# Attention masks: from matmuls into PSUM to one VectorE pass that adds the mask, takes the maximum and writes SBUF

## The chip, the cores and the metric

The kernel runs on one core of one Trainium2 chip. Five engines work side by side, each with an instruction queue of its own that runs in order: TensorE (PE in the profile, with its weight loads as PEld) multiplies matrices and writes PSUM; VectorE (DVE) and ScalarE (ACT) do elementwise work on SBUF and PSUM; GpSimd (POOL) does elementwise work on SBUF; SyncE (SP) issues the DMAs of this kernel. They tell each other with semaphores when a result is there or a buffer is free.

The metric is the time of one execution on the device in microseconds (us). Before the change the median of three runs is 2638.52 us, the lowest 2634.18 and the highest 2640.28.

## What is computed

The reference is a decoder trunk of two layers on 1024 tokens of width 1024. Layer 0 mixes with "native sparse attention" of 12 heads: each head attends in three branches, to all earlier tokens (with 16 blocks of 64 tokens and the 16 best taken, every block is selected, so only the causal mask is left), to a window of 512 tokens, and to 63 compressed blocks. Layer 1 mixes with forgetting attention, causal as well, with a decay that is added to the scores. In both layers 4 more heads attend to 256 memory tokens, with no mask. A gated convolutional feed-forward part follows in each layer. What the change touches is the masked softmax:

```python
def masked_softmax(s, mask):
    s = jnp.where(mask, s, NEG)
    s = s - jnp.max(s, axis=-1, keepdims=True)
    e = jnp.exp(s) * mask
    return e / jnp.maximum(jnp.sum(e, axis=-1, keepdims=True), 1e-30)
...
        s = jnp.einsum('btghd,bngd->bghtn', qc, kc).astype(jnp.float32) * scale
        p_cmp = masked_softmax(s, cmp_end[None, :] <= t[:, None])
...
        p = masked_softmax(s.reshape(B, G, HG, Q_BLOCK, n_top * L_SEL), m_sel)
...
        m_win = (s_pos[None, :] >= 0) & (s_pos[None, :] <= t[:, None]) & (t[:, None] - s_pos[None, :] < WINDOW)
        s = jnp.einsum('btghd,bsgd->bghts', qc, kw).astype(jnp.float32) * scale
        p = masked_softmax(s, m_win)
...
        s = s + dcum[:, :, lo:hi, None] - dcum[:, :, None, :hi]
        p = masked_softmax(s, jnp.arange(hi)[None, :] <= t[:, None])
```

## The kernel before, in words

The kernel is one class, Trunk, that issues the whole program, with an order written out by hand in `attention`; a scheduler below it may move instructions within an engine's queue as their operands allow. Numbers are kept in 32 bits; a product of full precision is made of three matmuls on high and low parts (`mm3`, lines 156 to 158; `split`, lines 81 and 82).

Attention goes head by head. A unit is one head and one half c of the tokens (512 queries, as four blocks of 128, counted by `ii`). A unit of layer 0 has three branches: the causal one (tile `ps`), the window (`pw`) and the compressed blocks (`pc`), whose scores are made together with the window's ("joint": 64 more columns behind the window's). A unit of layer 1 has the causal branch alone; a memory unit (`pm` in layer 0) has 256 unmasked columns for each of its four blocks.

A branch is cut into groups of query blocks that fit two PSUM banks, the tile `psa` of 1024 columns, of which there are two. For each group:

- `score` (line 301) multiplies queries and keys into `psa`. Where a mask is needed, one more matmul adds it: the identity (`identb`, bf16) as weights, and as moving operand a mask of zeros and -1e30: `caub` (causal, 128 columns), `winb` (far edge of the window, 128 columns), or `wcb` (the causal mask of the window's last block and the mask of the 64 compressed blocks, 192 columns). Blocks that need no mask get no such matmul.
- `maximum` (lines 314, 318, 320): VectorE takes the negated maximum of each row from PSUM, into `stat`. Four unmasked blocks of equal width go in one instruction (line 314).
- `exponent` (lines 334, 337): ScalarE reads the scores from PSUM, adds the negated maximum as a bias, takes the exponential and writes the probabilities to the SBUF tile `ps`, `pw` or `pc`. An accumulator gives the row sums (ACTIVATION_READ_ACCUMULATOR); those of `pc` are summed on VectorE at line 341.
- `normalise` (lines 346 to 361): one over the sum on VectorE, then the scaling of the probabilities on GpSimd in layer 0 and mostly on VectorE in layer 1.

The units are worked off in steps. In a step, `turn_p` transposes up to four 128x128 pieces of probabilities on PE (line 391) into one of the four `psb` banks, ScalarE copies them to `pt` (line 398), VectorE makes the low part (`lower_p`, line 401), and two steps later `value` multiplies them with the values (line 414). `pace` sets at which step each group of scores is begun: several steps ahead of the first step that needs it, and not before the step that last uses the tile of probabilities that it will write (`early`). The maximum and the exponential of a group come one step after its scores: the maximum before that step's transposes, the exponential behind them.

```python
            run(k, "max")
            if st:
                self.turn_p(ap, st)
            run(k, "exp")
            if st:
                self.lower_p(st)
            run(k, "norm")
            while items and items[0]["at"] <= k:
                begin(k, items.pop(0))
```

Between the steps, projections of later heads are interleaved on PE as filler (`advance`), in both layers.

## Time and profile before

| what | value |
|---|---|
| median of three runs | 2638.52 us |
| the profiled execution, as timed | 2643.03 us |
| its span, first to last instruction | 2640.9 us |
| granted TensorE clock, mean | 0.985 |
| scores, L301, last seen in layer 0 and layer 1 | at 652 us and 1850 us |
| reductions L318 from PSUM | 288 instructions, 200.6 us |
| reductions L320 from PSUM (64 columns) | 96 instructions, 20.4 us |
| exponentials and their sums, L334 | 260.1 us |

How to read the profile. A row of the grouped view has the line of the kernel, the engine, the operation, output and inputs by the program's names, the shapes and the count; behind the first bar stand the busy time in us and the mean of one in ns, and behind the second the idle time of the engine just before these instructions and what ended it. Matmuls are pipelined, so the duration of one is longer than the time by which the next one follows it. The chain of waits goes back from the last instruction to what released it, step by step, and its shares tell which engines' work stood in the way of the end. A row of the waits has the waiting engine and line, what it waited for, the us in total, the number of times and the longest. In the timeline a row has the start, the duration and the instruction, and in brackets the idle time before it.

### The profile page before, as it was taken

The page shows a single profiled execution, that of the slowest core. Times are in us where ns is not written, and L with a number is a line of the kernel's source. Part 1 is how long each engine was busy: PE and PEld are TensorE (multiplying, and loading weights), DVE is VectorE, ACT ScalarE, POOL GpSimd, SP SyncE. Part 2 cuts the span into 40 slices and gives each one's busy share as a digit, 9 for nine tenths or more (in the row PEclk, how much of TensorE's full clock was granted, in tenths as well). Part 3 has the DMA queues.
Part 4 walks back from the last instruction along what each step waited for, and adds up shares of the span by engine and source line. Part 5 has one row for each costly group of instructions (what it writes and reads, how often), then busy time and mean ns, then how long its engine had stood idle before and what let it go on. Part 6 is the DMA issues. An engine that isn't in the chain of part 4 may idle for free.

```text
span 2640.9 us, 36023 instructions
## 1 busy us (share of the span) xinstructions
PE 2506.7 (95%) x12642; PEld 2073.0 (78%) x12642; DVE 1881.6 (71%) x2822; ACT 1331.5 (50%) x2553; POOL 751.2 (28%) x616
## 2 busy tenths in 40 slices
PE   7899899988999999998999999999999999998998
PEld 6787777776877888886888988887777888886886
DVE  5757677878377787877765467778576877787765
ACT  4437576768245454544454356656334545443443
POOL 0105344445133545543000000000223555454000
PEclk9999999999999999999999999999999999999999
DMA  8473123334422323337434556656532333337523
GB/s 243 142 206 109 53 81 100 89 108 136 153 88 82 102 96 109 108 125 273 133 128 128 160 171 194 188 177 181 197 112 69 104 112 100 101 105 262 186 90 118
DMA packets 302702, 357.72 MB, mean 135 GB/s; under 512 B 37961, under 2 KB 183225, under 8 KB 302521
## 3 DMA queue, kind: packets, MB, share of 16 engines
q1 hardware_dynamic: 302520, 355.41, 42.8%
q8 instruction: 100, 1.64, 0.3%
q14 instruction: 82, 0.66, 0.1%
HBM read 245.55 MB, written 109.78 MB: 135 GB/s over the span
## 4 chain that ended last, share of the span: by engine, by line
PE 71%; DVE 9%; DMA 6%; ACT 6%; POOL 4%; issue 3%; SPq 1%; POOLq 0%; ACTq 0%; DVEq 0%
PE psa L156 11%; PE psa L157 11%; PE psa L158 11%; PE psb L156 8%; PE psb L158 8%; PE psb L157 8%; PE psa L301 5%; PE psb L414 4%; PE psb L391 3%; DVE pt L401 2%; DVE stat L318 2%; POOL gs L1350 1%; DMA hT<-in_w_down_dram 1%; ACT ps L334 1%; POOL pw L358 1%
## 5 line engine op out<-in xcount | busy, mean ns | idle before, releaser
L81 ACT ACTIVATE wh<-wr 128x512 fp32r<-128x512 f32 (+2 forms) x254 | 193.1, 765 | 353.9 <-PE psb L158 147.2
L82 DVE TENSOR_TENSOR wl<-wr,wh 128x512 fp32r<-128x512 f32 (+2 forms) x254 | 241.6, 955 | 165.5 <-ACT wh L81 164.8
L1335 DVE SCALAR_TENSOR_TENSOR v<-u,cw,v 128x1023 f32<-128x1023 f32 (+1 forms) x176 | 273.1, 1552 | 68.7 <-ACT v L1333 65.8
L401 DVE TENSOR_TENSOR pt<-psb,pt 128x512 fp32r<-128x512 f32 (+2 forms) x380 | 245.7, 657 | 87.2 <-ACT pt L398 84.6
L398 ACT ACTIVATE pt<-psb 128x512 fp32r<-128x512 f32 (+2 forms) x380 | 217.5, 583 | 130.9 <-PE psb L391 129.5
L1333 ACT ACTIVATE v<-u,cw 128x1024 f32<-128x1024 f32 x88 | 109.6, 1245 | 310.2 <-DVE u L1322 283.4
L414 PE MATMUL psb<-pt,vv 128*128 128x512 f32 (+2 forms) x864 | 232.2, 366 | 12.4 <-DVE pt L401 9.0
L156 PE MATMUL psa<-hT,wh 128*128 128x512 f32 x560 | 219.2, 392 | 5.3 <-DVE u L1296 5.3
L301 PE MATMUL psa<-kk,qq 128*128 128x512 f32 (+4 forms) x792 | 196.4, 359 | 25.0 <-ACT ps L334 14.7
L158 PE MATMUL psa<-hT,wl 128*128 128x512 f32 x560 | 218.6, 390 | 0.8 <-DVE wl L82 0.8
L157 PE MATMUL psa<-hT,wh 128*128 128x512 f32 x560 | 218.5, 390 | 0.0
L318 DVE TENSOR_REDUCE stat<-psa 128x1 f32<-128x640 f32 (+7 forms) x288 | 200.6, 714 | 21.5 <-PE psa L301 20.3
L334 ACT ACTIVATE ps<-psa,stat 128x128 f32<-128x128 f32 (+2 forms) x224 | 156.7, 706 | 59.6 <-DVE stat L318 53.7
L120 POOL TENSOR_TENSOR rs<-ss,consts 128x1 f32<-128x1 f32 x44 | 25.8, 588 | 516.3 <-DVE ss L118 378.0
L472 POOL TENSOR_TENSOR wr<-wr 128x512 f32<-128x512 f32 x32 | 42.3, 1323 | 440.7 <-DMA wr<-o 426.6
L414 PEld LDWEIGHTS psb<-pt,vv 128*128 128x128 f32 x864 | 141.4, 195 | 30.8 <-DVE pt L401 16.1
L301 PEld LDWEIGHTS psa<-kk,qq 128*128 128x128 f32 x792 | 125.8, 194 | 47.3 <-ACT ps L334 23.6
L156 PE MATMUL psb<-hT,wh 128*128 128x512 f32 x384 | 160.0, 417 | 2.2 <-DVE rt L607 1.8
L156 PE MATMUL psb<-wh 128*128 128x512 f32 x352 | 139.3, 396 | 20.7 <-ACT wh L81 20.6
L1237 POOL TENSOR_TENSOR ws<-wr 128x512 f32<-128x512 f32 x44 | 74.7, 1699 | 295.6 <-DMA wr<-in_w_up_dram 213.2
L391 PE MATMUL psb<-consts,ps 128*128 128x128 f32 x928 | 150.7, 280 | 8.1 <-DVE pt L401 4.9
L158 PE MATMUL psb<-hT,wl 128*128 128x512 f32 x384 | 151.7, 395 | 0.0
(285 smaller groups left out, 6853.1 us busy)
## 6 DMA issues: line engine op xcount, KB each, us to landing
wr<-in_w_up_dram SPq DMA_DIRECT2D x88, 512.0 KB
wr<-gd SPq DMA_DIRECT2D x154, 256.0 KB
gd<-v SPq DMA_DIRECT2D x88, 256.0 KB
gd<-gs SPq DMA_DIRECT2D x66, 256.0 KB
o<-ob SPq DMA_DIRECT2D x128, 128.0 KB
wr<-o SPq DMA_DIRECT2D x32, 512.0 KB
hT<-in_w_down_dram SPq DMA_DIRECT2D x64, 256.0 KB
qd<-st SPq DMA_DIRECT2D x56, 256.0 KB
```

The source lines that it names most:

```text
L81: nc.scalar.activation(hi, src, AF.Copy)
L82: nc.vector.tensor_tensor(lo, src, f32(hi), ALU.subtract)
L156: mm(out, lh, rh, start=first, stop=False, skip_group_check=more)
L157: mm(out, lh, rl, start=False, stop=False, skip_group_check=more)
L158: mm(out, ll, rh, start=False, stop=last, skip_group_check=more)
L301: nc.tensor.matmul(out, w, rhs, start=b not in banks[:i], stop=b not in banks[i + 1:])
L318: nc.vector.reduce_max(br["stat"][:, 0, ii:ii + 1], s[:, o:o + w], axis=AX.X, negate=True)
L391: nc.tensor.transpose(tp[0:kb, x:x + P], br["pt"][ii][:, o:o + kb], self.ident)
L398: nc.scalar.activation(st["hi"], st["src"], AF.Copy)
L401: self.nc.vector.tensor_tensor(st["lo"], st["src"], f32(st["hi"]), ALU.subtract)
L414: self.nc.tensor.matmul(out, v, t, start=st["begin"] and i == 0, stop=st["end"] and i == len(mms) - 1)
L1335: nc.vector.scalar_tensor_tensor(v[:, d:], u[:, :S - d], cw[:, tap, i:i + 1], v[:, d:], ALU.mult, ALU.add)
```

## The change

The mask matmuls and the identity in bf16 are gone. The masks become as wide as the scores: `caub` has 1024 columns, of which the first 896 are zero and the last 128 hold the causal mask, and a block of n columns takes its last n; `winb` has five blocks of 128 (far edge, three of zeros, causal); `cmpb` holds 64 columns for each of the eight query blocks.

A new function, `lift`, issues one VectorE operation for each query block and branch that has a mask: it adds score (PSUM) and mask (SBUF), multiplies by -1, writes the result to the tile of probabilities in SBUF, and takes the minimum along the row into `stat`, which is the negated maximum. In the instruction list of the changed kernel each of these is followed by a second VectorE instruction of 128x1 that writes `stat`. The exponential then reads the tile of probabilities and writes it in place, with a scale of -1 and the same bias. The tile of probabilities is therefore claimed in `maximum` and no longer in `exponent`. Memory units, without a mask, keep the reduction and the exponential from PSUM.

VectorE has 3207 instructions in the changed program (2822 before). PE has the same 12304 other matmuls, and 336 mask matmuls fewer.

```diff
@@ -90,21 +90,22 @@
         nc.sync.dma_start(c, a["consts"][:, 0:C_CAU])
         self.ident = c[:, C_ID:C_ID + P]
         self.rv = c[:, C_RV:C_RV + 1]
-        self.identb = cp.tile([P, P], BF16, name="identb")
-        nc.vector.tensor_copy(self.identb, self.ident)
-        self.m_cau = cp.tile([P, P], BF16, name="caub")
+
+        self.m_cau = cp.tile([P, S], BF16, name="caub")
+        nc.vector.memset(self.m_cau[:, :S - P], 0.0)
         self.nhalf = c[:, C_NH:C_NH + 1]
 
     def masks(self, pool, keep):
         nc, m = self.nc, pool.tile([P, C_TRI - C_CAU], F32, name="masks")
         nc.sync.dma_start(m, self.a["consts"][:, C_CAU:C_TRI])
-        nc.vector.tensor_copy(self.m_cau, m[:, 0:P])
-        self.m_win = keep.tile([P, P], BF16, name="winb")
-        nc.vector.tensor_copy(self.m_win, m[:, P:2 * P])
-
-        self.m_wc = keep.tile([P, NT, 192], BF16, name="wcb")
-        nc.vector.tensor_copy(self.m_wc[:, :, P:], m[:, 2 * P:].rearrange("p (t n) -> p t n", t=NT))
-        nc.vector.tensor_copy(self.m_wc[:, :, 0:P], m[:, 0:P].rearrange("p (o n) -> p o n", o=1).to_broadcast([P, NT, P]))
+        nc.vector.tensor_copy(self.m_cau[:, S - P:], m[:, 0:P])
+
+        self.m_win = keep.tile([P, 5 * P], BF16, name="winb")
+        nc.vector.memset(self.m_win[:, P:4 * P], 0.0)
+        nc.vector.tensor_copy(self.m_win[:, 0:P], m[:, P:2 * P])
+        nc.vector.tensor_copy(self.m_win[:, 4 * P:], m[:, 0:P])
+        self.m_cmp = keep.tile([P, NT, 64], BF16, name="cmpb")
+        nc.vector.tensor_copy(self.m_cmp, m[:, 2 * P:].rearrange("p (t n) -> p t n", t=NT))
 
     def gain(self, pool, row, bufs=1):
         g = self.sb(pool, [P, D], F32, "gb", bufs)
@@ -279,7 +280,7 @@
         nc, br, s = self.nc, it["br"], self.psa()
         it["s"] = s
         for ii, o, n in it["grp"]:
-            k0, k1, masks = br["spans"][ii]
+            k0 = br["spans"][ii][0]
             if "joint" in br:
                 f, t0 = n - 192, k0 // P
                 segs = [(o + f, o + n, lambda k: k[:, t0 + f // P, :])]
@@ -294,8 +295,6 @@
                     rhs = at(k)
                     out = s[:, b0:b1] if len(rhs.shape) == 2 else s[:, b0:b1].rearrange("p (t n) -> p t n", n=P)
                     mms.append((b0 // CH, out, q[:, ii * P:(ii + 1) * P], rhs))
-            for mo, mk in masks:
-                mms.append(((o + mo) // CH, s[:, o + mo:o + mo + mk.shape[1]], self.identb, mk))
             banks = [b for b, *_ in mms]
             for i, (b, out, w, rhs) in enumerate(mms):
                 nc.tensor.matmul(out, w, rhs, start=b not in banks[:i], stop=b not in banks[i + 1:])
@@ -309,34 +308,43 @@
             for i, b in enumerate(u["branches"]):
                 b["stat"] = u["stat"][:, :, 4 * i:4 * i + 4]
         br["same"] = len({k1 - k0 for k0, k1, _ in br["spans"].values()}) == 1
-        if br["same"] and len(grp) == 4:
-            n = grp[0][2]
-            nc.vector.reduce_max(br["stat"][:, 0, :], s[:, 0:4 * n].rearrange("p (i n) -> p i n", n=n), axis=AX.X, negate=True)
-        else:
-            for ii, o, n in grp:
-                w = n - 64 if joint else n
-                nc.vector.reduce_max(br["stat"][:, 0, ii:ii + 1], s[:, o:o + w], axis=AX.X, negate=True)
-                if joint:
-                    nc.vector.reduce_max(joint["stat"][:, 0, ii:ii + 1], s[:, o + w:o + n], axis=AX.X, negate=True)
-
-    def exponent(self, ap, it):
-        nc, br, s = self.nc, it["br"], it["s"]
-        joint = br.get("joint")
         if it["first"]:
             for b in (br, joint) if joint else (br,):
                 tag, width, bufs = b["p"]
                 b["pa"], b["pt"], b["len"] = self.sb(ap, [P, width], F32, tag, bufs), {}, 0
+        if br["spans"][0][2] is None:
+            n = grp[0][2]
+            nc.vector.reduce_max(br["stat"][:, 0, :], s[:, 0:4 * n].rearrange("p (i n) -> p i n", n=n), axis=AX.X, negate=True)
+            return
+        for ii, o, n in grp:
+            w = n - 64 if joint else n
+            self.lift(br, ii, s[:, o:o + w])
+            if joint:
+                self.lift(joint, ii, s[:, o + w:o + n])
+
+    def lift(self, br, ii, s):
+
+        w = s.shape[1]
+        p = br["pt"][ii] = br["pa"][:, br["len"]:br["len"] + w]
+        br["len"] += w
+        self.nc.vector.tensor_tensor_reduce(p, s, br["spans"][ii][2], -1.0, 3e38, ALU.add, ALU.min, br["stat"][:, 0, ii:ii + 1])
+
+    def exponent(self, ap, it):
+        nc, br, s = self.nc, it["br"], it["s"]
+        joint = br.get("joint")
         for ii, o, n in it["grp"]:
-            w = n - 64 if joint else n
-            p = br["pa"][:, br["len"]:br["len"] + w]
-            br["pt"][ii] = p
-            br["len"] += w
-            nc.scalar.activation(p, s[:, o:o + w], AF.Exp, bias=br["stat"][:, 0, ii:ii + 1], accum_out=br["stat"][:, 1, ii:ii + 1])
+            st = br["stat"]
+            if br["spans"][ii][2] is None:
+                p = br["pt"][ii] = br["pa"][:, br["len"]:br["len"] + n]
+                br["len"] += n
+                nc.scalar.activation(p, s[:, o:o + n], AF.Exp, bias=st[:, 0, ii:ii + 1], accum_out=st[:, 1, ii:ii + 1])
+                continue
+            p = br["pt"][ii]
+            nc.scalar.activation(p, p, AF.Exp, bias=st[:, 0, ii:ii + 1], scale=-1.0, accum_out=st[:, 1, ii:ii + 1])
             if joint:
-                p = joint["pt"][ii] = joint["pa"][:, ii * 64:(ii + 1) * 64]
-                nc.scalar.activation(p, s[:, o + w:o + n], AF.Exp, bias=joint["stat"][:, 0, ii:ii + 1])
-                joint["len"] += 64
-        if joint and joint["len"] == 256:
+                p = joint["pt"][ii]
+                nc.scalar.activation(p, p, AF.Exp, bias=joint["stat"][:, 0, ii:ii + 1], scale=-1.0)
+        if joint and it["last"]:
             joint["same"] = True
             nc.vector.reduce_sum(joint["stat"][:, 1, :], joint["pa"].rearrange("p (i n) -> p i n", i=4), axis=AX.X)
 
@@ -452,7 +460,8 @@
             for i, br in enumerate(scored):
                 early = max(b["early"] for b in (br, br.get("joint", br)))
                 due = next(k for k in range(u["start"], len(steps)) if any(q[0] is br for q in steps[k]["ps"])) - lead
-                its += [{"u": u, "br": br, "grp": g, "first": j == 0, "early": early, "due": due} for j, g in enumerate(self.groups(br))]
+                gs = self.groups(br)
+                its += [{"u": u, "br": br, "grp": g, "first": j == 0, "last": g is gs[-1], "early": early, "due": due} for j, g in enumerate(gs)]
                 its[-1]["norm"] = (i, len(brs) if br is scored[-1] else i + 1)
             its[0]["load"] = True
             items += its
@@ -545,7 +554,8 @@
 
     @staticmethod
     def causal(c, mask):
-        return {ii: (0, (c * 4 + ii + 1) * P, [((c * 4 + ii) * P, mask)]) for ii in range(4)}
+        n = [(c * 4 + ii + 1) * P for ii in range(4)]
+        return {ii: (0, n[ii], mask[:, S - n[ii]:]) for ii in range(4)}
 
     def mem_units(self, ap, qd, kv, tags, need, on):
         nc = self.nc
@@ -553,7 +563,7 @@
         for h in range(NMH):
             kv = {}
             for c in range(2):
-                br = {"spans": {ii: (0, NMEM, []) for ii in range(4)}, "kb": P, "gate": None, "p": tags[c], "on": on}
+                br = {"spans": {ii: (0, NMEM, None) for ii in range(4)}, "kb": P, "gate": None, "p": tags[c], "on": on}
 
                 def load(h=h, c=c, br=br, kv=kv):
                     if c == 0:
@@ -790,12 +800,12 @@
             vc = self.vc[:, g].rearrange("n s d -> n (s d)")
             for h in range(g * 6, g * 6 + 6):
                 for c in range(2):
-                    sp_c = {ii: (0, 64, []) for ii in range(4)}
+                    sp_c = {ii: (0, 64, self.m_cmp[:, c * 4 + ii, :]) for ii in range(4)}
                     sp_w = {}
                     for ii in range(4):
                         i = c * 4 + ii
                         k0 = max(0, i - 4) * P
-                        sp_w[ii] = (k0, (i + 1) * P, ([(0, self.m_win)] if i >= 4 else []) + [(i * P - k0, self.m_wc[:, i, :])])
+                        sp_w[ii] = (k0, (i + 1) * P, self.m_win if i >= 4 else self.m_cau[:, S - (i + 1) * P:])
                     brs = [{"spans": self.causal(c, self.m_cau), "kb": P, "p": t_s[c], "on": "pool"},
                            {"spans": sp_w, "kb": P, "p": t_w[c], "on": "pool"},
                            {"spans": sp_c, "kb": 64, "p": t_c, "on": "pool"}]
```

## The prediction

> **What bounds the kernel now.** I read the page's first part, then the busy time by stage, then in the two attention stages the chain that ended last and PE's waits.
>
> ```profile
> PE 2506.7 (95%) x12642; PEld 2073.0 (78%) x12642; DVE 1881.6 (71%) x2822; ACT 1331.5 (50%) x2553; POOL 751.2 (28%) x616
> ```
>
> PE (TensorE) is busy 95% of the span, but the change works only where scores are made, L301. These rows are layer 0's attention and layer 1's: the stretch, its length, busy us (and instructions) of PE, PE's weight loads, DVE, ACT, POOL, then granted clock, DMA share and GB/s:
>
> ```profile
> 190.00:672.00 482.00, 433.02 (x2739) 351.68 (x2738) 369.56 (x758) 336.96 (x852) 215.76 (x271) 0.98 0.34 97
> 1536.00:1870.00 334.00, 326.23 (x1823) 263.21 (x1822) 258.56 (x532) 213.13 (x524) 10.81 (x9) 0.98 0.63 181
> ```
>
> In layer 0 PE idles 482 - 433 = 49 us and DVE (VectorE) 112 us; in layer 1 PE idles 8 us, so there PE is the bound. The chains, layer 0 first, shares of the stage:
>
> ```profile
> by line: PE psa L301 14.2%; PE psb L391 10.7%; PE psb L414 10.5%; DVE pt L401 8.0%; issue 7.6%; DVE stat L318 7.0%; POOL pw L358 5.8%; ACT pw L334 5.3%; ACT pt L398 4.2%; ACT ps L334 3.2%; ACT pc L337 1.9%; PE psb L157 1.6%; DVE stat L346 1
> by line: PE psa L301 15.4%; PE psb L414 12.4%; PE psb L391 11.6%; PE psb L156 11.5%; PE psb L158 11.0%; PE psb L157 10.8%; ACT ps L334 4.2%; issue 3.2%; DVE stat L318 2.8%; DVE pt L401 2.8%; DVE ps L361 2.6%; ACT pt L398 1.9%; DMA qx<-qd 1.
> ```
>
> Layer 0 has no single bound: its chain changes hands between PE, DVE, ACT (ScalarE) and POOL. So I weigh each saved or added microsecond by the share of its line's busy time that lies on the chain. Busy time of L301, L318 and L334, each for layer 0 and then layer 1:
>
> ```profile
> 190.00:672.00 482.00, 173.18 (x952) 124.42 (x952) 0.98 0.34 97
> 1536.00:1870.00 334.00, 86.98 (x448) 61.09 (x448) 0.98 0.63 181
> 190.00:672.00 482.00, 131.34 (x192) 0.98 0.34 97
> 1536.00:1870.00 334.00, 69.31 (x96) 0.98 0.63 181
> 190.00:672.00 482.00, 167.34 (x449) 0.98 0.34 97
> 1536.00:1870.00 334.00, 92.78 (x256) 0.98 0.63 181
> ```
>
> PE scoring: 14.2% of 482 = 68.4 us of 173.2, weight 0.40; layer 1, 51.4 of 87.0, 0.59. DVE maxima: 33.7 of 131.3, 0.26; layer 1, 9.4 of 69.3, 0.13. ACT exponentials: 8.5% of 482 = 41.0 of 167.3, 0.24; layer 1, 14.0 of 92.8, 0.15. These weights are a choice: they hold while the chain keeps its shape.
>
> **Mask matmuls removed.** 336 matmuls with their weight loads go, 240 in layer 0 and 96 in layer 1:
>
> ```profile
> L301 PE MATMUL psa<-wcb,identb 128*128 128x192 bf16 x96 | 24.1, 251 | 0.0
> L301 PE MATMUL psa<-winb,identb 128*128 128x128 bf16 x48 | 11.0, 230 | 0.0
> L301 PE MATMUL psa<-caub,identb 128*128 128x128 bf16 x192 | 44.7, 233 | 0.0
> ```
>
> The first two are layer 0's; of the 192 causal ones each layer has 96. Their 230 to 251 ns are mostly pipeline. What PE can use is the distance between starts; in a timeline (start, duration) two projection matmuls of 512 columns stand 0.23 us apart:
>
> ```profile
> 410.05 0.40 PE L157 MATMUL psb<-hT,wh 128*128 128x512 f32 x1
> 410.28 0.40 PE L158 MATMUL psb<-hT,wl 128*128 128x512 f32 x1
> ```
>
> By columns that is 58 ns for 128 and 86 ns for 192: layer 0, 144 x 0.058 + 96 x 0.086 = 16.6 us; layer 1, 96 x 0.058 = 5.6 us. Weighted: 6.6 + 3.3 = 9.9 us gained. Bounds: nothing, if PE then waits elsewhere, to the full 22.2.
>
> **The score bank freed earlier.** A psa tile (two buffers) is held until ACT has read it; afterwards until DVE's pass, and ACT works in SBUF. PE's waits that this shortens, in layer 0 and then layer 1, with the wait nearest to them:
>
> ```profile
> PE psa L301 <- ACT ps L334: 13.2, 12, 2.5
> PE psa L301 <- ACT pc L337: 11.5, 13, 2.5
> PE psb L414 <- DVE pt L401: 10.8, 19, 2.4
> ...
> PE psa L301 <- ACT ps L334: 1.5, 5, 0.5
> ```
>
> They last about 1 us each. An exponential with its accumulator read takes about 0.8 + 0.1 us (timeline below), so nearly all of 24.7 + 1.5 us can go. What is late next is DVE's L401, for which the value matmuls already wait. Weighted: 24.7 x 0.40 + 1.5 x 0.59 = 10.8 us gained; bounds 0 to 26.2.
>
> **The VectorE pass.** 384 reductions (L318 and L320; 288 in layer 0, 96 in layer 1) become 384 add-and-minimum passes, and the built instruction list has a second DVE instruction, 128x1, behind each. By the Trainium skill's "VectorE: DVE Perf Modes", section "Two Vector instructions with no wait between them", an operation that also writes out its accumulator is two instructions; the list agrees. The pass reads PSUM and one SBUF tensor, as L401 does:
>
> ```profile
> L318 DVE TENSOR_REDUCE stat<-psa 128x1 f32<-128x1024 f32 x24 | 29.3, 1219 | 5.4 <-PE psa L301 5.3
> L318 DVE TENSOR_REDUCE stat<-psa 128x1 f32<-128x640 f32 x72 | 58.7, 815 | 2.4 <-PE psa L301 2.0
> L318 DVE TENSOR_REDUCE stat<-psa 128x1 f32<-128x512 f32 x36 | 24.5, 680 | 0.4 <-PE psa L301 0.2
> L318 DVE TENSOR_REDUCE stat<-psa 128x1 f32<-128x128 f32 x36 | 10.1, 279 | 5.8 <-PE psa L301 5.8
> L401 DVE TENSOR_TENSOR pt<-psb,pt 128x512 fp32r<-128x512 f32 x320 | 215.3, 683 | 77.3 <-ACT pt L398 75.5
> L201 DVE SCALAR_TENSOR_TENSOR wl<-wr,gc,wh 128x128 fp32r<-128x128 f32 x112 | 33.6, 344 | 8.3 <-ACT wh L200 8.1
> L334 ACT ACTIVATION_READ_ACCUMULATOR ps<-psa,stat 128x1 f32 x224 | 46.1, 206 | 0.0
> ```
>
> At 512 elements L401 takes 683 ns against the reduction's 680: the pass itself costs nothing more, which I take; a fused form of three operands is 344 against 279 at 128, so up to +0.065 us. A gain is excluded, as both stream each element once. DVE's read has no row. Its bounds are the fixed part of a DVE slot and ACT's whole read row, 0.206:
>
> ```profile
> 401.11 0.83 DVE L318 TENSOR_REDUCE stat<-psa 128x1 f32<-128x640 f32 x1
> 401.85 0.21 DVE L320 TENSOR_REDUCE stat<-psa 128x1 f32<-128x64 f32 x1
> ...
> 402.18 0.80 ACT L334 ACTIVATE pw<-psa,stat 128x640 f32<-128x640 f32 x1 [1.82 <-DVE stat L320]
> ...
> 402.88 0.19 ACT L334 ACTIVATION_READ_ACCUMULATOR pw<-psa,stat 128x1 f32 x1
> 402.97 0.59 ACT L398 ACTIVATE pt<-psb 128x512 fp32r<-128x512 f32 x1
> ```
>
> The slope between 640 and 1024 elements is 404/384 = 1.05 ns, so of the 0.74 us slot at 401.11 the fixed part is 0.07: the lower end. ACT's read holds its engine 0.09 us, from 402.88 to 402.97, and I take that, as the same kind of instruction. On the chain: (288 x 0.26 + 96 x 0.13) x 0.09 = 87 x 0.09 = 7.9 us lost; ends 6.1 and, at 0.206 + 0.065 = 0.27, 24.
>
> The Trainium skill's "Vector Engine (DVE) Microarchitecture Reference", section "Measured stream behaviour on trn2 (trn3 not measured)", gives about 75 ns per DVE instruction after queue overlap, near the row's 0.07; by it this term would be an estimated 6.5 us.
>
> No new wait is added for the scores. The pass also writes the probability tile, which an earlier unit's transposes must have left; these stand on PE ahead of the score matmuls. Behind the pass in DVE's queue wait L401 and L346; for L401 wait PE's value matmuls L414 and the psb buffers of the transposes L391.
>
> **The exponential from SBUF.**
>
> ```profile
> L398 ACT ACTIVATE pt<-psb 128x512 fp32r<-128x512 f32 x320 | 190.1, 605 | 107.2 <-PE psb L391 106.3
> L81 ACT ACTIVATE wh<-wr 128x512 fp32r<-128x512 f32 x170 | 106.3, 630 | 255.0 <-PE psa L158 100.5 <-PE psb L158 86.4 <-DMA wr<-gd 34.4
> L1333 ACT ACTIVATE v<-u,cw 128x1024 f32<-128x1024 f32 x88 | 109.6, 1245 | 310.2 <-DVE u L1322 283.4 <-POOL ws L1245 13.7 <-issue 11.6
> L334 ACT ACTIVATE ps<-psa,stat 128x1024 f32<-128x1024 f32 x24 | 26.9, 1122 | 6.6 <-DVE stat L318 6.5
> ```
>
> A copy from SBUF takes 630 ns, from PSUM 605: +0.025, taken as the pair with like work. The far pair, 1245 against 1122, gives +0.12, the upper end; the lower is 0. On the chain 288 x 0.24 + 96 x 0.15 = 84 exponentials: 2.1 us lost, ends 0 and 10. The memory-attention units keep the old path. The setup trades a few mask copies and memsets outside the attention stages; no DMA is added or removed. I take both at nothing: PE's projection work before 190 us covers them, and uncovered it is about one L318 row of 1.2 us.
>
> **Sum.** -9.9 - 10.8 + 7.9 + 2.1 = -10.7 us against the profiled execution's 2643.0 (span 2640.9 and 2.1 around it). That execution lies 4.5 above the median, so I subtract from the median: 2638.5 - 10.7 = 2628.
>
> **Rivals.**
>
> *Larger gain.* PE sets the pace throughout, masks and psa waits come off whole: 22.2 + 26.2, less 6.1 on DVE: -42, so 2596. For it: PE's 95%. Against it: PE has only 40% of layer 0's scoring on the chain. Chance 0.12.
>
> *The wait moves.* PE no longer waits for psa but for L401 (the 10.8 us row) by as much: -9.9 + 7.9 + 2.1 = 0, so 2639. For it: DVE works in order. Against it: DVE idles 112 us. Chance 0.15.
>
> *DVE becomes layer 0's bound: slower.* DVE idles 63 us more than PE there; 63/288 = 0.22 us per pass is the point from which DVE is the fuller engine. Then the PE gains of layer 0 are void, and DVE's added time takes PE's weight: at 0.27, 288 x 0.27 x 0.40 = 31, plus 96 x 0.27 x 0.13 = 3.4, plus 2.1, less layer 1's 3.3: +33, so 2672; at 0.22, 2665. For it: ACT's read row of 206 ns, L201's 344, and that no such pass has a row here. Against it: reads overlap on ACT. Chance 0.32.
>
> *The pass runs at half rate: slower.* Layer 0 makes 12 x 8960 masked scores per partition and layer 1 12 x 4608 (from the spans). At 1.05 ns more each that is 113 and 58 us; with 26 us of reads layer 0's DVE would be busy 370 + 113 + 26 = 509 us of 482. That is 27 us past the stage without a single wait; I add three quarters of the 49 us that PE waits there now, since the handoffs stay: +64, so 2702.
>
> ```profile
> L134 DVE SCALAR_TENSOR_TENSOR xn<-xl,rs,gb 128x1024 f32<-128x1024 f32 x12 | 15.4, 1283 | 6.2 <-POOL rs L120 6.2
> ```
>
> Against it: this row with two f32 SBUF tensors takes 1283 ns, not twice 1219. Chance 0.05. The skill's microarchitecture page, section "Points that are easy to get wrong", says that such an operation halves its throughput with two non-bf16 SBUF sources; the row disagrees, and the new pass has PSUM and a bf16 mask.
>
> **How the numbers follow.** Forecast 0.36 (2628, by itself 2618 to 2633), larger gain 0.12, moved wait 0.15, DVE bound 0.32, half rate 0.05. So faster 0.48, same 0.15, slower 0.37; 0.2% is 5.3 us, about what a measurement here tells from no change. The range runs from near the larger gain, 2600, to 2669, inside the DVE-bound case; half rate is left out.
>
> **What would show it.** Right: PE's L301 waits no longer for ACT; the pass at 640 elements takes 0.80 to 0.85 us and its read holds DVE under 0.1; layer 0's attention loses about 7 us, layer 1's about 3. Wrong: a pass and read together over 0.2 us longer than the reduction; PE idle in layer 0 growing at L414 and L391 behind L401; or exponentials over 0.1 us longer.

## The result and the profile after

| | time, us (median, lowest to highest) | ratio to before, 95% interval |
|---|---|---|
| before | 2639.40 (2634.18 to 2640.44) | |
| after | 2606.44 (2605.36 to 2610.82) | 0.9882 [0.9864, 0.9900] |

The changed kernel is faster by 33 us, where 10.7 were forecast. The execution profiled took 2605.37 us, its span 2602.7.

The first part of the page after, busy us, share of the span and number of instructions of each engine:

```profile
PE 2466.1 (95%) x12306; PEld 2058.2 (79%) x12306; DVE 1887.8 (73%) x3207; ACT 1342.2 (52%) x2553; POOL 751.8 (29%) x616
```

PE still shows 95%: its busy time fell with the span, by 40.6 us, and it has 336 instructions fewer (12642 to 12306). Where, the busy time by stage of the kernel after says, layer 0's attention first (columns as in the prediction: the stretch, its length, then busy us of PE, its weight loads, DVE, ACT and POOL, granted clock, DMA share, GB/s):

```profile
189.50:647.50 458.00, 405.39 (x2492) 338.46 (x2491) 373.78 (x1046) 344.61 (x852) 214.82 (x271) 0.99 0.34 101
1508.60:1829.60 321.00, 313.13 (x1723) 260.98 (x1723) 256.94 (x627) 215.23 (x522) 10.42 (x8) 0.99 0.65 188
```

The prediction's row of layer 0 before begins 2 us ahead of the first score matmul. From the first score matmul to the last value matmul, as in the rows after, it is:

```profile
192.00:673.00 481.00, 431.96 (x2733) 350.50 (x2732) 370.17 (x758) 336.96 (x852) 215.76 (x271) 0.98 0.34 96
```

Layer 0's attention lost 23 us (481 to 458), layer 1's 13 (334 to 321; its row before has 4 instructions more than the 96 masks account for, under 1 us). What lies between and around them changed by under 3 us. PE's busy time fell by 26.6 us (431.96 to 405.39) and 13.1 us (326.23 to 313.13), 39.7 in all, while its idle time in layer 0 is 458 - 405.4 = 52.6 us against 49.0 before. For 336 mask matmuls that is 0.12 us each, against the 58 or 86 ns by columns of the prediction. So in the balance the time came out of PE's work, not out of its waits; the experiments show that this balance hides two changes of the waits that run against each other.

The chain that ended last in layer 0's attention after, shares of the stage:

```profile
by line: PE psa L300 11.3%; PE psb L399 10.6%; PE psb L422 10.1%; issue 9.7%; DVE pt L409 9.6%; POOL pw L366 6.4%; ACT pt L406 5.7%; DVE ps L330 4.4%; ACT pw L343 4.1%; DVE pw L330 2.3%; DVE stat L354 2.2%; ACT ps L343 2.0%; ACT pc L346 1.8
```

(L300 is the line L301 of before, L399 is L391, L422 is L414, L409 is L401, L343 is L334; the passes are L330.) The chain still changes hands. PE's scoring went from 14.2% of 482, 68 us, to 11.3% of 458, 52 us. The passes have 4.4 + 2.3 = 6.7%, much like the maxima's 7.0% before.

PE's waits in layer 0's attention after (us in total, times, longest):

```profile
PE psa L300 <- DVE stat L330: 12.1, 11, 2.6
PE psb L422 <- DVE pt L409: 9.4, 11, 1.9
PE psb L399 <- DVE pt L409: 8.6, 10, 2.2
...
PE psa L300 <- DVE stat L355: 2.8, 1, 2.8
```

No wait of a score matmul for ACT is left, in layer 1 neither. But 12.1 + 2.8 = 14.9 us of waits for `psa` remain in layer 0, now for DVE, where 24.7 stood.

The groups of the pass, of its accumulator read and of the exponential (count, then busy us and mean ns of one, then idle time before it):

```profile
L330 DVE CUSTOM_DVE_ANT_0 ps<-psa,caub 128x1024 f32<-128x1024 f32 x24 | 29.2, 1218 | 4.7 <-PE psa L300 4.6
L330 DVE CUSTOM_DVE_ANT_0 pw<-psa,winb 128x640 f32<-128x640 f32 x48 | 39.2, 816 | 1.4 <-PE psa L300 1.3
L330 DVE DVE_READ_ACCUMULATOR2_ANT stat<- 128x1 f32 x384 | 31.6, 82 | 0.0
L343 ACT ACTIVATE ps<-ps,stat 128x1024 f32<-128x1024 f32 x24 | 27.6, 1148 | 7.8 <-DVE stat L330 7.8
```

The pass takes what the reduction took: 1218 ns against 1219 at 1024 elements, 816 against 815 at 640. The exponential from SBUF takes 1148 against 1122, +26 ns. The read has a row of 82 ns; whether it costs DVE that much is to be seen in DVE's timeline after (start, duration):

```profile
242.08 1.23 DVE L330 CUSTOM_DVE_ANT_0 ps<-psa,caub 128x1024 f32<-128x1024 f32 x1 [0.16 <-PE psa L300]
243.23 0.08 DVE L330 DVE_READ_ACCUMULATOR2_ANT stat<- 128x1 f32 x1
243.23 1.28 DVE L409 TENSOR_TENSOR pt<-psb,pt 128x512 fp32r<-128x512 f32 x2
```

The read and the next instruction have the same start. The rows of e6 below confirm that the read takes no slot of its own: there a pass of 640 elements starts at 246.58 and the instruction behind its read at 247.33, 0.75 us later, where the reduction of before held DVE 0.74 us (401.11 to 401.85 in the prediction).

Where PE's time per mask comes from is seen in a timeline of PE and its weight loads before, in layer 1, at the last score matmul of a unit and the projections behind it:

```profile
1602.66 0.40 PE L301 MATMUL psa<-ky,qx 128*128 128x512 f32 x1
...
1602.89 0.10 PEld L301 LDWEIGHTS <-identb 128*128 128x128 bf16 x1 [0.28 <-issue]
1602.89 0.23 PE L301 MATMUL psa<-caub,identb 128*128 128x128 bf16 x1
1602.90 0.20 PEld L156 LDWEIGHTS psb<-hT,wh 128*128 128x128 f32 x1
1602.93 0.48 PE L156 MATMUL psb<-hT,wh 128*128 128x512 f32 x1
...
1603.25 0.39 PE L157 MATMUL psb<-hT,wh 128*128 128x512 f32 x1
```

and at the same kind of place after:

```profile
1572.30 0.57 PE L300 MATMUL psa<-ky,qx 128*128 128x384 f32 x2
1572.48 0.19 PEld L157 LDWEIGHTS psb<-hT,wh 128*128 128x128 f32 x1
...
1572.70 0.39 PE L157 MATMUL psb<-hT,wh 128*128 128x512 f32 x1
...
1572.93 0.40 PE L158 MATMUL psb<-hT,wh 128*128 128x512 f32 x1
```

The mask matmul holds only 0.04 us between starts (1602.89 to 1602.93). But the 512-column matmul behind it has 0.32 to the next start, not 0.23: its own weights, 0.20 us to load, begin to load 0.03 before it starts. After, that load begins 0.22 us before its matmul (1572.48 against 1572.70) and is hidden under the last score matmul, and the distance is 0.23. So a mask costs 0.04 + 0.09 = 0.13 us of PE here; the busy times above, over all 336, say 0.12. Why the load comes so late is not shown: the load of the identity itself begins only with the mask matmul (1602.89), after 0.28 us in which the profile shows nothing that it waited for. The masks are in bf16 and their neighbours in f32, and no run tried a mask in f32.

### The profile page after: what moved, and what is told of

It reads as the page before. It is cut to its first block, busy times and chain, and to the rows that moved or that the text cites. A ratio compares the mean times of both kernels' runs of the same rounds, so it can differ in the third digit from the quotient of the medians.

```text
span 2602.7 us, 35727 instructions
## 1 busy us (share of the span) xinstructions
PE 2466.1 (95%) x12306; PEld 2058.2 (79%) x12306; DVE 1887.8 (73%) x3207; ACT 1342.2 (52%) x2553; POOL 751.8 (29%) x616
## 4 chain that ended last, share of the span: by engine, by line
PE 71%; DVE 10%; ACT 6%; DMA 5%; POOL 4%; issue 3%; SPq 0%; POOLq 0%; ACTq 0%; DVEq 0%
PE psa L157 12%; PE psa L158 12%; PE psa L159 12%; PE psb L157 9%; PE psb L159 9%; PE psb L158 8%; PE psa L300 3%; PE psb L399 3%; PE psb L422 3%; DVE pt L409 2%; ACT pt L406 1%; POOL gs L1360 1%; DVE ps L330 1%; POOL pw L366 1%; DVE wl L82 1%
## 5 line engine op out<-in xcount | busy, mean ns | idle before, releaser
L1345 DVE SCALAR_TENSOR_TENSOR v<-u,cw,v 128x1023 f32<-128x1023 f32 (+1 forms) x176 | 283.1, 1608 | 68.7 <-ACT v L1343 68.5
L409 DVE TENSOR_TENSOR pt<-psb,pt 128x512 fp32r<-128x512 f32 (+2 forms) x380 | 246.6, 658 | 62.1 <-ACT pt L406 59.0
L422 PE MATMUL psb<-pt,vv 128*128 128x512 f32 (+2 forms) x864 | 225.8, 356 | 17.3 <-DVE pt L409 13.2
L300 PE MATMUL psa<-kk,qq 128*128 128x512 f32 (+4 forms) x792 | 186.1, 350 | 20.1 <-DVE stat L330 12.3
L343 ACT ACTIVATE ps<-ps,stat 128x128 f32<-128x128 f32 (+1 forms) x192 | 147.8, 771 | 56.8 <-DVE stat L330 56.3
L422 PEld LDWEIGHTS psb<-pt,vv 128*128 128x128 f32 x864 | 141.4, 191 | 42.2 <-DVE pt L409 21.7
L121 POOL TENSOR_TENSOR rs<-ss,consts 128x1 f32<-128x1 f32 x44 | 25.8, 588 | 511.2 <-DVE ss L119 372.5
L399 PE MATMUL psb<-consts,ps 128*128 128x128 f32 x928 | 149.2, 279 | 14.5 <-DVE pt L409 7.5
L157 PE MATMUL psb<-hT,wh 128*128 128x512 f32 x384 | 156.6, 408 | 1.0 <-DVE pt L409 0.9
L1247 POOL TENSOR_TENSOR ws<-wr 128x512 f32<-128x512 f32 x44 | 67.7, 1539 | 295.3 <-DMA wr<-in_w_up_dram 276.2
L158 PE MATMUL psb<-hT,wh 128*128 128x512 f32 x384 | 150.8, 393 | 0.0
L300 PEld LDWEIGHTS psa<-kk,qq 128*128 128x128 f32 x792 | 121.6, 194 | 36.1 <-DVE stat L330 13.8
```

What stands on the lines that cost most here:

```text
L157: mm(out, lh, rh, start=first, stop=False, skip_group_check=more)
L158: mm(out, lh, rl, start=False, stop=False, skip_group_check=more)
L300: nc.tensor.matmul(out, w, rhs, start=b not in banks[:i], stop=b not in banks[i + 1:])
L343: nc.scalar.activation(p, p, AF.Exp, bias=st[:, 0, ii:ii + 1], scale=-1.0, accum_out=st[:, 1, ii:ii + 1])
L399: nc.tensor.transpose(tp[0:kb, x:x + P], br["pt"][ii][:, o:o + kb], self.ident)
L409: self.nc.vector.tensor_tensor(st["lo"], st["src"], f32(st["hi"]), ALU.subtract)
```

## The experiments

e1 to e4, e5 to e7 and e8 to e10 each ran on one chip, beside runs of the kernel before. The changed kernel itself came out at 33.0 and, in e10, 28.5 us under before; differences of 4 to 5 us between two sets are therefore not read as an effect. (Its granted clock was 0.986 to 0.988 in the first four runs and 0.983 to 0.986 in e10.)

**e1: the mask matmuls left out of the kernel before.** Bank and exponential stay as they were; the scores are not masked.

```diff
-            for mo, mk in masks:
-                mms.append(((o + mo) // CH, s[:, o + mo:o + mo + mk.shape[1]], self.identb, mk))
```

> The kernel before with its 336 mask matmuls left out (so the masks are left out of the result); reduction and exponential from PSUM as before. Theory A (a mask costs PE about 0.12 us, because the next weight load is no longer hidden, and PE sets the pace): 336 x 0.12 = 40 us less, so 2598 to 2607. Theory B (the gain comes from the score bank that VectorE frees earlier; masks are worth only the 10 us of the prediction): about 2629. Theory C (both half): about 2620.

Measured: 2617.36 us, ratio 0.9915 [0.9898, 0.9931], 21.4 us faster. Layer 0's attention, then PE's waits for `psa` there:

```profile
193.30:657.70 464.40, 410.81 (x2492) 342.62 (x2491) 367.42 (x758) 337.52 (x852) 215.52 (x271) 0.97 0.35 99
```

```profile
PE psa L299 <- ACT pc L335: 16.8, 15, 3.9
PE psa L299 <- ACT ps L332: 10.5, 12, 2.0
```

That is nearest to theory C. The masks alone are worth twice the forecast of 9.9, and two thirds of the whole gain. PE's busy time in the whole program fell by 32.0 us (2506.7 to 2474.7), or 0.095 us for each mask, and the span of the profiled execution by 25.8 (2640.9 to 2615.1), so 6.2 us turned into idle time: in layer 0 PE idles 464.4 - 410.8 = 53.6 us instead of 49.0, and its waits for ACT at `psa` grew from 24.7 to 27.3.

**e2: the mask matmuls put back into the changed kernel,** 336 of the old shapes, with masks of zeros, which add nothing.

```diff
+            zero = []
+            if "joint" in br:
+                zero = ([(o, P)] if n == 5 * P + 64 else []) + [(o + n - 192, 192)]
+            elif br["spans"][ii][2] is not None:
+                zero = [(o + n - P, P)]
+            for z, w in zero:
+                mms.append((z // CH, s[:, z:z + w], self.identb, self.m_cau[:, 0:w]))
```

> The changed kernel with 336 matmuls of the identity and a zero mask put back behind the scores, at the places and widths of before. Theory A: all of the gain goes, 2634 to 2645. Theory B: the gain of the freed bank stays, about 2616. Theory C: about 2625.

Measured: 2638.41 us, ratio 0.9998 [0.9988, 1.0007]. All of the gain is gone, as theory A had it, although the bank is still freed by the pass. Layer 0's attention and its waits:

```profile
189.70:671.40 481.70, 430.69 (x2732) 350.93 (x2731) 373.17 (x1046) 345.03 (x852) 215.21 (x271) 0.97 0.34 96
```

```profile
PE psb L431 <- DVE pt L418: 14.0, 17, 2.2
PE psb L408 <- DVE pt L418: 10.2, 12, 2.1
PE psa L309 <- DVE stat L339: 9.2, 9, 1.7
```

With the bank freed PE waits 9.2 us for `psa`, not 24.7; but its waits for the DVE step between transposes and value matmuls (here L418) grew, at the value matmuls from 10.8 to 14.0 and at the transposes from 5.5 to 10.2. PE's idle time is 51.0 us, as much as before. That is the mechanism of the rival "the wait moves", as long as the masks are there.

**e3: the kernel before with each mask matmul cut to its first 32 columns.** The mask's other columns are left out.

```diff
-                mms.append(((o + mo) // CH, s[:, o + mo:o + mo + mk.shape[1]], self.identb, mk))
+                mms.append(((o + mo) // CH, s[:, o + mo:o + mo + 32], self.identb, mk[:, 0:32]))
```

> The kernel before with every mask matmul cut to its first 32 columns (the rest of the masks is left out of the result). If a mask costs by its columns, as the prediction sized it (58 ns for 128), three quarters and more of its cost goes: 8 us less if weighted, 17 to 30 us less if PE sets the pace, so 2609 to 2631. If it costs by its weight load (theory A), nothing or a few us: 2633 to 2640.

Measured: 2636.97 us, ratio 0.9986 [0.9975, 0.9997], 1.8 us faster. Its timeline of PE and the weight load, at the place shown above:

```profile
1601.02 0.19 PE L301 MATMUL psa<-caub,identb 128*128 128x32 bf16 x1
1601.02 0.20 PEld L156 LDWEIGHTS psb<-hT,wh 128*128 128x128 f32 x1
1601.05 0.47 PE L156 MATMUL psb<-hT,wh 128*128 128x512 f32 x1
...
1601.37 0.39 PE L157 MATMUL psb<-hT,wh 128*128 128x512 f32 x1
```

With a quarter or a sixth of the columns the distances are nearly the same, 0.03 and 0.32. So the price of a mask is not its columns. The load of the next weights begins 0.03 us before its matmul here too (1601.02 and 1601.05).

**e4: the kernel before with each mask matmul issued twice,** with which -1e30 becomes -2e30.

```diff
-            for mo, mk in masks:
+            for mo, mk in masks + masks:
```

> The kernel before with every mask matmul issued twice. The second stands behind the first as wcb stands behind winb, 67 ns apart in the trace of before, so if PE sets the pace (theory A) 336 x 0.067 = 22 us more, about 2661; with the weights of the prediction (0.40 and 0.59) about 10 us more, 2649; under theory B no more than 5.

Measured: 2660.06 us, ratio 1.0080 [1.0065, 1.0095], 21.3 us slower. The timeline of PE there:

```profile
1613.97 0.28 PE L301 MATMUL psa<-caub,identb 128*128 128x128 bf16 x2
1614.07 0.48 PE L156 MATMUL psb<-hT,wh 128*128 128x512 f32 x1
1614.38 0.39 PE L157 MATMUL psb<-hT,wh 128*128 128x512 f32 x1
```

Two masks hold 0.10 us where one held 0.04, and the next distance is 0.31 as with one. So at this place a second mask costs 0.06 us, what the columns say, though its weights are loaded once more (12978 loads against 12642); the first one costs twice that. The time rose by 21.3 us, which is theory A's 22, and PE's busy time in the whole program by 15.7 (2506.7 to 2522.4): work added to PE reached the end in full, and a few us of new idle time with it.

**e5: the changed kernel with the exponentials reading PSUM again,** so that ACT holds the bank as before. The masks in SBUF are zeros: the scores are not masked.

```diff
-            nc.scalar.activation(p, p, AF.Exp, bias=st[:, 0, ii:ii + 1], scale=-1.0, accum_out=st[:, 1, ii:ii + 1])
+            w = p.shape[1]
+            nc.scalar.activation(p, s[:, o:o + w], AF.Exp, bias=st[:, 0, ii:ii + 1], accum_out=st[:, 1, ii:ii + 1])
```

> The changed kernel with its exponentials reading the scores from PSUM again (VectorE still writes its sum to SBUF and takes the minimum there; all masks are zero, so they are left out of the result). The score bank is held until ScalarE has read it. If the 11 us by which the changed kernel beats the kernel before without its mask matmuls (2606 against 2617) come from the bank that is freed earlier: 2614 to 2620. If they come from VectorE's pass itself or the order of the queues: 2603 to 2609.

Measured: 2621.57 us, ratio 0.9931 [0.9905, 0.9956]. Layer 0's attention and its waits for `psa`:

```profile
189.50:656.90 467.40, 408.78 (x2492) 340.21 (x2491) 372.96 (x1046) 337.90 (x852) 215.83 (x271) 0.98 0.35 98
```

```profile
PE psa L300 <- ACT pc L347: 18.8, 18, 3.7
PE psa L300 <- ACT ps L344: 13.1, 12, 2.6
```

That is 15.1 us over the changed kernel (11.0 over e10): the worth of the freed bank, less what the exponential from SBUF costs, once the masks are gone. It is 1.6 us above what was expected if the bank is the cause, and 12 above the other case. Without the freed bank, 31.9 us of waits for ACT stand at `psa`. Against e1, which has the old reductions and no second DVE instruction, e5 is 4.2 us slower; pass and read together cost at most about that, which is no more than two sets differ by (e8 is a closer test).

**e6: one more DVE instruction behind each pass,** a copy of one PSUM column, 384 in all.

```diff
+        self.spare_n = (self.spare_n + 1) % 32
+        self.nc.vector.tensor_copy(self.spare[:, self.spare_n:self.spare_n + 1], s[:, 0:1])
```

> The changed kernel with one more VectorE instruction behind each of the 384 passes: a copy of one PSUM column of the scores into a spare tile, a slot of about 0.07 us, as long as the accumulator read's. With the weights of the prediction (0.26 and 0.13): 87 x 0.07 = 6 us more, 2612. If PE alone sets the pace: 2606 to 2608. If VectorE is close to the bound of layer 0: 288 x 0.07 x 0.4 and more, 2616 or above.

Measured: 2604.66 us, ratio 0.9862 [0.9840, 0.9884]: no slower than the changed kernel. The group of the copies and the stage of layer 0, then some rows of DVE's timeline:

```profile
L333 DVE COPY spare<-psa 128x1 f32<-128x1 f32 x384 | 57.9, 151 | 0.1
190.50:643.60 453.10, 403.20 (x2492) 336.80 (x2491) 385.17 (x1334) 345.50 (x852) 216.48 (x271) 0.99 0.36 102
```

```profile
246.58 0.82 DVE L331 CUSTOM_DVE_ANT_0 pw<-psa,winb 128x640 f32<-128x640 f32 x1
247.33 0.08 DVE L331 DVE_READ_ACCUMULATOR2_ANT stat<- 128x1 f32 x1
247.33 0.15 DVE L333 COPY spare<-psa 128x1 f32<-128x1 f32 x1
247.40 0.21 DVE L331 CUSTOM_DVE_ANT_0 pc<-psa,cmpb 128x64 f32<-128x64 f32 x1
```

A copy holds DVE 0.07 us. By the prediction's weights that is 87 x 0.07 = 6 us of time; none is seen, and layer 0's stage is 453.1 long, no longer than without the copies (458.0, and 460.0 in e10). DVE, busy 385.2 us of it, has that much slack there.

**e7: value matmuls of layer 1 three steps behind their transposes instead of two,** with a fourth buffer for them, to take away waits behind DVE's L409.

```diff
-        self.n_pt, self.n_q = 3, 1
+        self.n_pt, self.n_q = 4, 1
...
-            return self.attention(ap, 1, od, units, work, 5)
+            return self.attention(ap, 1, od, units, work, 5, 4, 3)
```

> The changed kernel with the value matmuls of layer 1 three steps behind the transposes instead of two, and four pt buffers instead of three. PE's waits for L409 in layer 1's attention (4.6 us) can go. If PE's waits are what is left there: 2602 to 2605. If they move to another place: 2606 or more.

Measured: 2610.81 us, ratio 0.9890 [0.9867, 0.9914]: no gain. The waits moved: those of the value matmuls behind L409 fell from 4.6 to 0.9 us, but the transposes now wait for the scaling of the probabilities, where 0.3 us stood:

```profile
PE psb L399 <- DVE ps L369: 6.4, 2, 4.7
```

The same in layer 0, where most of the waits are, was not tried.

**e8: both e2 and e5,** the changed kernel with zero-mask matmuls and with exponentials from PSUM; the scores are not masked.

> The changed kernel with the 336 matmuls of identity and zero mask put back and the exponentials reading PSUM again (all masks zero, so they are left out of the result): masks on PE, VectorE's pass, bank held. Against 2638.4 with masks and the freed bank (e2): if the freed bank is worth 15 us with masks too, as it is without them (2621.6 against 2606.4), 2653; if it is worth less while PE still makes the masks, 2638 to 2646. Against 2621.6 without masks and with the bank held (e5), the masks are worth 21 us if they cost what they cost in e1: 2643.

Measured: 2640.87 us, ratio 1.0002 [0.9992, 1.0012]. Layer 0's attention, and its waits:

```profile
190.90:671.20 480.30, 432.49 (x2732) 350.76 (x2731) 372.00 (x1046) 336.57 (x852) 215.66 (x271) 0.98 0.34 96
```

```profile
PE psa L309 <- ACT ps L353: 13.2, 12, 2.6
PE psb L432 <- DVE pt L419: 11.7, 20, 2.2
PE psa L309 <- ACT pc L356: 10.3, 13, 2.5
PE psb L409 <- DVE pt L419: 4.6, 11, 1.0
```

With masks on PE and the bank held by ACT, e8 differs from the kernel before by the pass and its read alone (and by the zeros). Their price is therefore 0.02% of the time, with an interval from -2 to 3 us. With this run there are four kernels that all make the VectorE pass:

| | bank held by ACT | bank freed by the pass | worth of the bank |
|---|---|---|---|
| mask matmuls in: time | 2640.9 (e8) | 2638.4 (e2) | 2.5 |
| mask matmuls out: time | 2621.6 (e5) | 2606.4 (after), 2610.5 (e10) | 15.1, 11.0 |
| worth of the masks | 19.3 | 32.0, 27.9 | |
| PE idle in layer 0, masks in | 47.8 | 51.0 | |
| PE idle in layer 0, masks out | 58.6 | 52.6 (after), 53.7 (e10), 48.4 (e7) | |

The two gains do not add: together they are worth 30 to 35 us, one by one 19.3 + 2.5 = 22, and the 2.5 is no more than two sets differ by. PE's idle time in layer 0 is length less busy time. e7 has the changed kernel's code in layer 0, so three profiles of that code can be compared; the rows of e10 and e7:

```profile
190.40:650.40 460.00, 406.27 (x2492) 339.48 (x2491) 374.29 (x1046) 344.70 (x852) 214.84 (x271) 0.98 0.36 100
189.70:649.40 459.70, 411.26 (x2492) 343.69 (x2491) 370.71 (x1046) 344.57 (x853) 216.01 (x271) 0.97 0.35 101
```

PE is busy 405.4, 406.3 and 411.3 us for the same work, at a granted clock of 0.99, 0.98 and 0.97, so single rows of busy or idle time carry some 5 us of scatter. Without the freed bank, taking the masks out makes PE idle 10.8 us more, and the waits for ACT at `psa` grow from 23.5 to 31.9; with it, between 2.6 less and 2.7 more. And with the masks in, the freed bank only turns waits at `psa` (23.5 to 9.2) into waits behind DVE (11.7 + 4.6 = 16.3 to 14.0 + 10.2 = 24.2). The idle times differ by 8 to 13 us, the times by 8.6 to 12.7. But with the kernel before and e1 in place of e8 and e5 the removal made PE idle only 4.6 us more, so the idle times show the direction and not the size. Why the waits behind DVE do not grow in the same way once the masks are out (9.4 + 8.6 = 18.0 us after) stays open.

**e9: memory units through the pass as well,** with a zero mask, so that their bank, too, is freed by DVE.

```diff
-                br = {"spans": {ii: (0, NMEM, None) for ii in range(4)}, "kb": P, "gate": None, "p": tags[c], "on": on}
+                br = {"spans": {ii: (0, NMEM, self.m_cau[:, 0:NMEM]) for ii in range(4)}, "kb": P, "gate": None, "p": tags[c], "on": on}
```

> The changed kernel with the memory units, which have no mask, sent through the same VectorE pass with a mask of zeros, so that their score bank is freed by VectorE too: 16 reductions of 1.2 us become 64 passes of about 0.41 + 0.08 us, 12 us more of VectorE, and 16 bank waits of up to 1 us end earlier. If the freed bank is what counts: 2598 to 2606. If VectorE's extra time counts: 2607 to 2615.

Measured: 2614.53 us, ratio 0.9902 [0.9885, 0.9918], against 2610.54 of e10 beside it: 4 us slower or the same, no gain. One reduction over four blocks becomes four passes, and there was no mask matmul to save.

**e10: the changed kernel once more,** beside e8 and e9.

> The changed kernel itself, unchanged, timed beside the other two on the same chip: 2605 to 2610.

Measured: 2610.54 us, ratio 0.9890 [0.9875, 0.9904]. No version tried is faster than the changed kernel beyond the spread; e6, 1.8 us under it, does more work, and the two intervals overlap.

## Why the prediction was right and wrong

The direction and the range were right; the size was not. 10.7 us were forecast, 33.0 were measured (28.5 in e10). The measured 2606.4 lies 12 us below what the forecast's own case allowed, 2618 to 2633, and 10 above the "larger gain" of 2596; the range held only because its lower end was drawn near that rival, whose terms were wrong in size too. By its steps:

**Mask matmuls removed: the step that failed.** "By columns that is 58 ns for 128 and 86 ns for 192" sized the term at 22.2 us full and 9.9 weighted. e3 shows that columns are not the price, and the timelines show what is: 0.04 us for the matmul and about 0.09 for the load that it uncovers. By PE's busy time in the whole program the full term is 31 to 41 us, 0.09 to 0.12 for each mask: 32.0 from before to e1, 30.8 from e8 to e5 (2505.1 to 2474.3), 38.5 from e2 to after (2504.6 to 2466.1), 40.6 from before to after. At 0.12 the weights of the prediction make of it 240 x 0.12 x 0.40 + 96 x 0.12 x 0.59 = 18.3 us, at 0.09 some 14; e1 measured 21.4, e8 to e5 19.3. So the duration was 1.4 to 1.8 times too small, and with the bank held the weights were about right or up to a third too low. The prediction took the distance between two matmuls of 512 columns and scaled it down. In the same trace of before stood matmuls of 128 columns, the transposes:

```profile
1615.76 0.60 PE L391 MATMUL psb<-consts,ps 128*128 128x128 f32 x4
1616.67 0.38 PE L391 MATMUL psb<-consts,ps 128*128 128x128 f32 x2
```

Four take 0.22 us more than two, 0.11 each, not 0.058. That was the row to use. The Trainium skill's "TensorE: Matmul & The Clock Gate", section "Back-to-back issue gap", says that the spacing of small matmuls is set by the weight load too, and gives about 81 ns at 128 columns against 56 by columns alone; the runs agree in kind and show 0.09 to 0.12 us for a lone mask and 0.06 for a second one with the same weights (e4).

**Weights.** They come nearest for the removal with the bank held, and fail for the two others. Work added to PE counted in full (e4: 15.7 us more of PE's busy time, 21.3 of time; at 0.06 each the weights say 9). And with the bank freed the masks are worth 28 to 32 us of time for 35.5 to 38.5 of PE's busy time (e2 to e10 and to after). A share of the chain belongs to one edit at a time: after one limit is gone, the other's share is another.

**The score bank freed earlier.** Forecast 10.8; measured 11.0 to 15.1 with the masks out, but 2.5 with them in (e8 to e2). The mechanism was right as named: PE no longer waits for ACT at `psa`. That nearly all of the 24.7 us can go was not: 14.9 remain, for DVE. What the rival "the wait moves" describes happens in e2, where the masks are still there, and not in the changed kernel.

**The VectorE pass.** That the pass costs no more than the reduction was right to 1 ns. The read has a row of 82 ns, near the 0.09 taken, but holds up nothing: the next instruction starts with it. The term of 7.9 us is 3 at most with the masks on PE (e8 against before) and 4.2, no more than two sets differ by, without them (e5 against e1), and e6 shows that a slot of 0.07 us per pass, charged at 0.26 in layer 0, would not have reached the end either. The Trainium skill's "Vector Engine (DVE) Microarchitecture Reference", section "Measured stream behaviour on trn2 (trn3 not measured)", has about 75 ns per DVE instruction: the copies of e6 agree with their 0.07, the read does not.

**The exponential from SBUF.** +26 ns measured at 1024 elements against the 25 taken. Its worth on the chain, 2.1 us, was not measured by itself; it is within the 11.0 to 15.1 us of the bank.

**Where the missing 22 us are.** Along the path before, e8, e5, after: the pass cost -2 to 3 us where 7.9 were charged, the masks gave 19.3 where 9.9 were counted, and the bank with its exponentials 11.0 to 15.1 where 10.8 - 2.1 = 8.7 were. So the masks' term is the largest miss, 9.4 us, on this path; with the bank freed first it would be 18 or more.

**The rivals.** "Larger gain" (2596) had PE's pace throughout as its reason, and that is nearest to what the runs show: but its 22.2 us for the masks were too small (31 to 41 by PE's busy time), and of its 26.2 us of waits 14.9 stayed under another name. "DVE becomes layer 0's bound" asked for 0.22 us more per pass; the pass brought none, and e6, which adds a third of that, lost nothing; up to 0.22 it was not tried. "Half rate" would have shown 1.6 us at 640 elements; it is 0.816.

**What would show it.** The three signs named as right came (no wait for ACT, 0.816 us, read under 0.1), and yet the stages lost 23 and 13 us where about 7 and 3 were named. The sign named as wrong, PE idling more behind L401, came only weakly: 10.8 to 9.4 at the value matmuls, 5.5 to 8.6 at the transposes.

## What to carry to other kernels

Price a short matmul that has weights of its own by the distances between starts around it, before and behind, not by its columns or its row: here a mask of 0.04 us made the next distance 0.09 us longer, with 128 columns and with 32. Where two limits lie side by side (PE's pace and a held bank), try the edits in all four combinations before crediting either: here the bank was worth 2.5 or 11 to 15 us, according to the masks. An idle time that stays the same while the stage gets shorter does not say that no wait was removed: here it was 49.0 us before and 52.6 after, but 58.6 with the masks out and the bank still held.

## What the runs showed of the hardware

- One bf16 mask matmul of 128 columns, with an identity as weights, between f32 matmuls costs 0.13 us of PE at the place shown and 0.09 to 0.12 on average; 0.09 of it comes with the next matmul's weight load, which begins only 0.03 us ahead. With 32 columns it is nearly the same, and a second mask with the same weights costs 0.06.
- The accumulator read behind a fused DVE pass has a row of 82 ns and no slot: at 243.23, and at 247.33 in e6, the next instruction starts with it, and a pass of 640 elements with its read holds DVE 0.75 us, the reduction 0.74.
- A fused add, scale and minimum from PSUM with a bf16 mask from SBUF, written to SBUF in f32, runs as fast as the plain reduction from PSUM: 1218 against 1219 ns at 1024 elements.
- The same PE work in layer 0 was busy 405.4, 406.3 and 411.3 us at a granted clock of 0.99, 0.98 and 0.97 (after, e10, e7).
